# Seven block products for v of the second token group, computed ahead of the attention

## The chip, the cores and the metric

One Trainium2 (trn2) chip, one core. The metric is the device time of one launch in microseconds; the kernel before takes 2644.64 us (median of 3 runs, 2640.68 to 2646.3).

## The reference

One layer of a bidirectional encoder over 1024 prompt tokens and 256 sample tokens (1280 rows of `D_MODEL` = 2048), all in fp32:

```python
hn = rmsnorm(x, norm_w)
proj = hn @ w_in                    # 9232 columns
# na_q, na_k, na_v, na_g: 1024 each; ml_qk: 2048; ml_v, ml_o, ml_z: 1024 each; 16 gate columns
att = neighbourhood_attention(na_q, na_k, na_v, na_rpb)      # 8 heads x 128, grid 64 wide, window 8 x 16
att = att * silu(na_g)
...
ml = bidirectional_mlstm(q, k, ml_v, gates)                  # 4 heads x 256, chunks of 64
...
y = x + concat(att, ml) @ w_out
out = rmsnorm(y, final_w)
```

What matters here are the 2048 columns of v (`na_v` and `ml_v`) and the 16 gate columns, for the second part of the tokens.

## The kernel before, in words

**Precision.** Every large product is made of three matmuls on a split operand: `hi` is a cast (ScalarE, L153), `lo` the rest (VectorE, L154), and hi.hi, hi.lo and lo.hi are summed in PSUM. So each tile of weights costs one ScalarE and one VectorE instruction before TensorE can use it.

**Tokens.** The 1280 tokens form two groups: group 0 with 768 (`GA`), group 1 with 512 (`GB`).

**Stages.** The *first stage* projects group 0: `pair_a` (L328) makes two blocks of 128 output columns by seven block products (a Strassen scheme) with 384 token columns, and GpSimd makes the four weight sums that the scheme needs (products 6, 3, 7 and 5; function `summed` in `pair_a`; tile names like `A60t`, four buffers). Eight of the pairs are v. Free time of GpSimd goes to the sums of `w_out` (`wsum`, stored to `sD`). The *second stage* projects group 1 by ordinary products: `proj_pair` (L503; 96 matmuls of 512 token columns to a pair, PSUM tiles `pc`, weight pieces `wr`, split tiles `ws`) for q, k, gates and the mLSTM columns, and `proj_v` (L565; 192 matmuls of 256 v columns to a unit, PSUM tiles `pv`, outputs `vo`) for the eight units of v. Unit 4 carries the 16 gate columns besides, in matmuls of 272 columns. The *output stage* multiplies with `w_out`, again by seven products (groups S, G00, G01, G10, G11 in the profile), and normalizes.

**Order of the second stage.** The loop at L1170 takes one head group `i` of four after the other: `proj_v(4 + i)`, two mLSTM pairs, `proj_v(i)`, the q and k pairs, and then, by `run`, the mLSTM and attention units of that group (names `mlp3...` for the prompt's mLSTM head 3, `nap7...` for the prompt's attention head 7, `nas...` and `mls...` for the sample). `run` gives its instructions a high priority; a scheduler fixes the order of each engine when the kernel is built, and puts the low-priority projections of later groups into the attention's gaps. Behind the loop come the late gates: for `ch` in 0, 2, 4, 6 `late_gate(OT0 + ch, 8 + ch)` (pairs 40 and 48, 42 and 50, 44 and 52, 46 and 54) followed by `build` of the output stage's operands (`bd0...`, split into `cm0...`), and then `late_gate(GT0 + h, h)` (pairs 16, 18, 20, 22). A late gate multiplies its columns into `mixT` (`mx...`), where the attention and the mLSTM have stored their outputs.

**Queues.** SyncE (SP) issues nearly all loads and stores in program order, one behind the other; a store that waits for its data holds all loads behind it.

```python
for i in range(ML_H):
    proj_v(4 + i, X)
    if i == 0:
        x_stats(1, lambda c: mid(f"xdg1_{c}", 256))
    for n in (QK0 + 8 + 2 * i, QK0 + 2 * i):
        proj_pair(n, X)
    ...
    proj_v(i, X)
    for n in (QT0 + 2 * i, KT0 + 2 * i):
        proj_pair(n, X)
    run(...)
```

Of the kernel before, what the change touches and what calls it, by code (L numbers as in the profile page):

```python
# [11 lines left out]
ALU = mybir.AluOpType  # L12
# [20 lines left out]
BIAS_S = 6 * NAK  # L33
XFIRST = (0, 1, 8, 9, 2, 3, 10, 11, 4, 5)
QT0, KT0, GT0, QK0, OT0, ZT0 = 0, 8, 16, 24, 40, 48
# [3 lines left out]
def kernel(  # L39
# [6 lines left out]
    w_o: bass.AP,  # L46
    w_os: bass.AP,
    lnw: bass.AP,
    rpb_tab: bass.AP,
# [20 lines left out]
    pT = [dram.tile([P, TT], F32, tag=f"pT{n}", name=f"pT{n}") for n in range(NCH)]  # L70
    vD = [dram.tile([TT, 256], F32, tag=f"vD{u}", name=f"vD{u}") for u in range(NU)]
    mixT = [dram.tile([P, TT], F32, tag=f"mx{k}", name=f"mx{k}") for k in range(KT)]
# [106 lines left out]
    rbs = [xa.tile([P, GA], F32, tag="rstdb0", name="rstdb0"), None]  # L179
    XSLOT = {2: (0, 0), 3: (0, 1), 6: (1, 0), 5: (1, 1), 4: (2, 0), 7: (2, 1)}  # L180

# [13 lines left out]
    def wsa(name):  # L195
        return wa.tile([P, 2, 256], F32R, tag="wsa", name=name, bufs=NWS)
# [131 lines left out]
    def pair_a(n1, bg=iter(()), hook=None, units={}):  # L328
# [32 lines left out]
        for r in range(4):  # L361
# [8 lines left out]
            def summed(i, x, y_, op):  # L370
                t = wa.tile([P, 256], F32, tag="wt", name=f"{nm}t{r}{i}", bufs=NWT)
                G.tensor_tensor(t, x, y_, op=op)
# [110 lines left out]
    def po(name):  # L483
        return wb.tile([P, 520], F32, tag="po", name=name, bufs=NPO)
# [79 lines left out]

    def proj_v(u, X):  # L565
        gates = u == NA_H // 2
        w = 272 if gates else 256
        nt = GB // P
        if gates:
            outs = [bank("a", f"pv{u}_{i}")[:, :w] for i in range(nt)]  # L570
        else:
            pb = [bank("pr", f"pv{u}_{i}") for i in range(nt // 2)]
            outs = [pb[t // 2][:, (t % 2) * 256 : (t % 2) * 256 + 256] for t in range(nt)]
        for r in range(4):
            raw = w_piece(w_in[NCH // 2 + u, r], f"v{u}_{r}")
            rawv = raw.rearrange("p (j f q c) -> p f q j c", j=2, f=2, q=2)
            if gates:
                graw = wb.tile([P, 2, 2, 16], F32, tag="wgr", name=f"wg{r}", bufs=2)
                DM.dma_start(
                    graw, w_g.rearrange("p (f r q c) -> p f r q c", f=2, r=4, q=2)[:, :, r]  # L580
                )
            for f_ in range(2):
                t = wb.tile([P, 2, 544], F32R, tag="wsp", name=f"wsv_{u}_{r}_{f_}", bufs=4)
                t4 = t[:, :, : 2 * w].rearrange("p h (k c) -> p h k c", k=2)
                h2, l2 = (
                    t4[:, z, :, 0:256].rearrange("p q (j c) -> p q j c", j=2) for z in range(2)
                )
                split(h2, l2, rawv[:, f_])
                if gates:
                    split(t4[:, 0, :, 256:272], t4[:, 1, :, 256:272], graw[:, f_])  # L590
                for tt in range(nt):
                    for q in range(2):
                        first, last = r + f_ + q == 0, r == 3 and f_ == 1 and q == 1
                        xh, xl = X.get(8 * f_ + 2 * r + q)
                        for m, (xs, wi) in enumerate(((xh, 0), (xh, 1), (xl, 0))):
                            PE.matmul(  # L596
                                outs[tt],
                                xs[:, tt * P : (tt + 1) * P],
                                t[:, wi, q * w : (q + 1) * w],
                                start=first and m == 0 and (gates or tt % 2 == 0),  # L600
                                stop=last and m == 2 and (gates or tt % 2 == 1),
                            )
        rc = rcs[1]
        for tt in range(nt):
            o = po(f"vo{u}_{tt}")[:, :256]
            S.mul(o, outs[tt][:, :256], rc[:, tt : tt + 1])
            r0 = GA + tt * P
            DM.dma_start(vD[u][r0 : r0 + P, :], o)
            if gates:
                V.scalar_tensor_tensor(  # L610
                    gt[:, GA // P + tt, :], outs[tt][:, 256:272], rc[:, tt : tt + 1], gb_sb,
                    op0=ALU.mult, op1=ALU.add,
                )

# [531 lines left out]

    class LazyX:
        def __init__(self):
            self.t = {}

        def get(self, k):
            if k not in self.t:
                self.t[k] = x_split(x_raw(wb, 520, "po", NPO, 1, k), k, 1)
            return self.t[k]

    def run(*streams):
# [10 lines left out]

    X = LazyX()
    rbs[1] = late.tile([P, GB], F32, tag="rstdb1", name="rstdb1")
    for i in range(ML_H):  # L1170
        proj_v(4 + i, X)
        if i == 0:
# [18 lines left out]
    WBLK = {1: (0, 0), 4: (1, 1), 2: (0, 1)}  # L1191
    WSUM = {6: 0, 3: 1, 7: 2, 5: 3}

# [135 lines left out]

    def add(o, a_, b_):  # L1330
        V.tensor_tensor(o, a_, b_, op=ALU.add)

    PARTS = {
# [83 lines left out]
def _layout(inputs):  # L1417
# [8 lines left out]
    for name, n in (("q", 1024), ("k", 1024), ("v", 1024), ("g", 1024), ("qk", 2048),  # L1426
# [6 lines left out]
        ch.reshape(2, 4, 2, P, nb // 2, 2, P).transpose(4, 1, 3, 5, 0, 2, 6).reshape(nb // 2, 4, P, 1024)  # L1433
    )
    gorder = [d * 8 + w_ * 4 + h for w_ in range(2) for d in range(2) for h in range(4)]
    w_g = np.ascontiguousarray(
# [13 lines left out]
    def table(qr, qc, kr, kc, rows):  # L1450
# [22 lines left out]
        "w_o": w_o,  # L1473
        "w_os": w_os,
        "lnw": np.ascontiguousarray(g["ln_w"][0].reshape(KT, P).T),
        "rpb_tab": tab,
# [30 lines left out]
```

## Time and profile before

| what | us |
|---|---|
| median of 3 runs | 2644.64 |
| the profiled execution | 2650.84 |
| its span in the trace | 2649.1 |
| TensorE busy | 2592.8 |
| VectorE busy | 1989.0 |
| ScalarE busy | 1386.2 |
| GpSimd busy | 819.0 |
| first stage | 0 to 1122 |
| second stage | 1122 to 2224 |
| output stage | 2224 to 2649 |

The granted TensorE clock of the profiled execution is 0.996. The stage borders are the starts of the first matmul on `pv` and of the first on `G00p`. A busy time counts matmuls to their modelled ends, so that TensorE can be shown busy while it waits a little between two matmuls; its pace is better read from the chain, which gives the number of matmuls in each uninterrupted piece.

### The profile page before, as it was taken

How to read it: one execution, taken by the hardware profiler on the slowest of the kernel's cores; microseconds unless marked ns; L12 is line 12 of the kernel's file. 1: busy time of each engine (PE TensorE's matmuls, PEld its weight loads, DVE VectorE, ACT ScalarE, POOL GpSimd, SP SyncE). 2: the span in 40 equal slices, each digit the busy share in tenths (PEclk: the TensorE clock that was granted, in tenths of full speed). 3: DMA queues.
4: the chain of work that ended last, by engine and by line, in shares of the span. 5: the costliest groups of instructions: out<-in, count | busy, mean ns of one | idle time of the engine just before them, and what ended most of it. 6: DMA issues, size and time to landing. Idle time of an engine off the chain costs nothing.

```text
span 2649.1 us, 43618 instructions
## 1 busy us (share of the span) xinstructions
PE 2592.8 (98%) x14518; PEld 2372.1 (90%) x14518; DVE 1989.0 (75%) x3962; ACT 1386.2 (52%) x3140; POOL 819.0 (31%) x1021
## 2 busy tenths in 40 slices
PE   8999999999999999999999999999999999999997
PEld 8899999999999999988999998989888878877786
DVE  7868878897879798874587587587567675787775
ACT  7534434444444444443566566576566443565654
POOL 0546565756566565410011011011011000124312
PEclk9999999999999999999999999999999999999999
DMA  6524344434343343544555656656555456778875
GB/s 209 180 92 147 124 156 134 158 97 171 106 148 123 126 148 117 184 133 143 189 163 184 197 162 191 188 161 186 170 172 168 157 171 227 227 252 307 288 221 179
DMA packets 245753, 454.20 MB, mean 171 GB/s; under 512 B 30320, under 2 KB 121624, under 8 KB 245528
## 3 DMA queue, kind: packets, MB, share of 16 engines
q1 hardware_dynamic: 232856, 407.38, 48.0%
q0 software_dynamic: 9216, 33.56, 3.6%
q10 hardware_dynamic: 3456, 10.49, 1.0%
q8 instruction: 114, 1.87, 0.3%
q14 instruction: 111, 0.91, 0.1%
HBM read 368.41 MB, written 82.91 MB: 170 GB/s over the span
## 4 chain that ended last, share of the span: by engine, by line
PE 47%; DMA 5%; DVE 3%; ACT 2%; issue 1%; POOL 1%; SPq 0%; ACTq 0%; POOLq 0%; DVEq 0%
PE pc L514 20%; PE pv L596 4%; PE G00p L1286 3%; PE G11p L1286 3%; PE S L1286 2%; PE G10p L1286 2%; PE G01p L1286 1%; PE A54b L190 1%; PE A52b L190 1%; DMA wr<-in_w_in_dram 1%; PE nap_1s L638 1%; PE nap_0s L638 1%; DMA nap_0vr<-vD 1%; DMA wrG10w<-sD 0%; PE mlp_2in L942 0%
## 5 line engine op out<-in xcount | busy, mean ns | idle before, releaser
L154 DVE TENSOR_TENSOR ws<-wr,ws 128x512 fp32r<-128x512 f32 x224 | 155.2, 697 | 115.0 <-ACT ws L153 114.2
L153 ACT CAST ws<-wr 128x512 fp32r<-128x512 f32 x224 | 137.5, 619 | 158.2 <-PE pc L514 118.3
L1309 POOL TENSOR_TENSOR y<-y,fn 128x512 f32<-128x512 f32 x40 | 62.5, 1577 | 413.5 <-ACT jk L1308 216.9
L104 POOL TENSOR_SCALAR mls_0r<-mls_0r 128x2 f32<-128x2 f32 x4 | 1.1, 277 | 255.7 <-ACT mls_0jk L1110 255.7
L154 DVE TENSOR_TENSOR ws_S<-wrS,ws_S 128x512 fp32r<-128x512 f32 x64 | 54.8, 884 | 15.6 <-ACT ws_S L153 15.4
L154 DVE TENSOR_TENSOR wsv<-wr_v,wsv 128x512 fp32r<-128x512 f32 x64 | 44.5, 698 | 21.4 <-ACT wsv L153 20.9
L153 ACT CAST wsv<-wr_v 128x512 fp32r<-128x512 f32 x64 | 39.3, 617 | 36.1 <-PE pc L514 21.9
L154 DVE TENSOR_TENSOR ws_G10w<-wrG10w,ws_G10w 128x512 fp32r<-128x512 f32 x56 | 45.2, 830 | 13.5 <-ACT ws_G10w L153 13.2
L1286 PE MATMUL S<-ws_S,xsb 128*128 128x512 f32 x192 | 48.3, 406 | 5.0 <-DVE ws_S L154 3.9
L153 ACT CAST ws_G11w<-wrG11w 128x512 fp32r<-128x512 f32 x56 | 34.6, 620 | 33.2 <-PE G11p L1286 16.4
L154 DVE TENSOR_TENSOR ws_G11w<-wrG11w,ws_G11w 128x512 fp32r<-128x512 f32 x56 | 43.0, 793 | 11.2 <-ACT ws_G11w L153 11.2
L154 DVE TENSOR_TENSOR ws_G01w<-wrG01w,ws_G01w 128x512 fp32r<-128x512 f32 x56 | 45.1, 828 | 7.9 <-ACT ws_G01w L153 6.7
L1286 PEld LDWEIGHTS S<-ws_S,xsb 128*128 128x128 f32 x192 | 36.8, 194 | 15.7 <-DVE ws_S L154 6.0
L167 DVE TENSOR_TENSOR pco<-pc,rstdb 128x512 f32<-128x512 f32 x48 | 32.9, 687 | 23.5 <-PE pc L514 23.4
L153 ACT CAST ws_S<-wrS 128x512 fp32r<-128x512 f32 x64 | 37.9, 617 | 20.6 <-PE S L1286 11.5
L276 DVE SCALAR_TENSOR_TENSOR pcv<-pco,cw_sb,pcv 128x516 f32<-128x516 f32 x64 | 47.7, 754 | 0.9 <-ACT pcv L270 0.8
L319 POOL DMA_DIRECT2D wsum<-in_w_os_dram x32 | 18.5, 577 | 96.4 <-DVE xg L161 77.5
L514 PE MATMUL pc<-x_2h,ws 128*128 128x512 f32 x112 | 44.8, 400 | 2.2 <-ACT ws L153 1.1
L153 ACT CAST ws_G10w<-wrG10w 128x512 fp32r<-128x512 f32 x56 | 33.9, 619 | 24.7 <-PE G10p L1286 11.0
L153 ACT CAST ws_G01w<-wrG01w 128x512 fp32r<-128x512 f32 x56 | 34.2, 618 | 22.7 <-PE G01p L1286 12.4
L153 ACT CAST ws_G00w<-wrG00w 128x512 fp32r<-128x512 f32 x48 | 29.4, 620 | 31.0 <-PE G00p L1286 17.3
L154 DVE TENSOR_TENSOR ws_G00w<-wrG00w,ws_G00w 128x512 fp32r<-128x512 f32 x48 | 36.3, 775 | 12.4 <-ACT ws_G00w L153 11.7
(1824 smaller groups left out, 9342.7 us busy)
## 6 DMA issues: line engine op xcount, KB each, us to landing
wr<-in_w_in_dram SPq DMA_DIRECT2D x112, 512.0 KB
wsum<-in_w_os_dram POOLq DMA_DIRECT2D x32, 512.0 KB, 4.4
sD<-wsum POOLq DMA_DIRECT2D x32, 512.0 KB, 3.3
wr_v<-in_w_in_dram SPq DMA_DIRECT2D x32, 512.0 KB
wrS<-in_w_o_dram SPq DMA_DIRECT2D x64, 256.0 KB
xq<-in_xtok_dram SPq DMA_DIRECT2D x20, 512.0 KB
xr<-in_xtok_dram SPq DMA_DIRECT2D x40, 256.0 KB
wrG00w<-sD SPq DMA_DIRECT2D x32, 256.0 KB
```

The costliest lines, as they stand in the source:

```text
L104: E.tensor_scalar(out, ssum, 1.0 / count, EPS, op0=ALU.mult, op1=ALU.add)
L153: S.copy(hi, src)
L154: V.tensor_tensor(lo, src, f(hi), op=ALU.subtract)
L167: V.tensor_tensor(o, src, rb, op=ALU.mult)
L190: PE.matmul(o, w(a_), x(b_), start=first and m == 0, stop=last and m == 2)
L276: V.scalar_tensor_tensor(dst[:, a:n], src[:, a + j - pad : n + j - pad], cw_sb[:, ct, j : j + 1], dst[:, a:n], op0=ALU.mult, op1=ALU.add,)
L319: G.dma_start(raw, w_os[u])
L514: PE.matmul(pb[j], t[:, wi, c : c + P], xs, start=r == 0 and f_ == 0 and q == 0 and wi == 0 and xs is xh, stop=r == 3 and f_ == 1 and q == ...
L596: PE.matmul(outs[tt], xs[:, tt * P : (tt + 1) * P], t[:, wi, q * w : (q + 1) * w], start=first and m == 0 and (gates or tt % 2 == 0), stop ...
L638: PE.matmul(b[:, :nkeys], qs(a_), ks(b_), start=i == 0, stop=i == 2)
L1286: PE.matmul(bk[s_], x_[:, xi, s_ * P : (s_ + 1) * P], t[:, wi, :512], start=first and m == 0, stop=last and m == 2,)
L1309: G.tensor_tensor(yc, yc, fn[nb], op=ALU.mult)
```

## The change: what it does

`proj_v` is gone. Its work is done in a new stage between the first stage and the loop, by seven block products over two column groups `cp` of 1024 columns:

- The first stage's v pairs store the four weight sums that GpSimd makes anyway to `sV` (128 stores of 128 KB through SP's queue).
- `v_build`, eight times, loads two tiles of x again, scales them (ScalarE), makes the token sums of the scheme with four instructions on GpSimd, and splits them.
- `v_product`, 7 x 2 times, runs 48 matmuls of 512 columns (tiles named `V` with group and product). Products 1, 4 and 2 read plain weights from a new input `w_vb`, which holds the same weights in this order; 6, 3, 7 and 5 read `sV`.
- `v_fold` adds the products, `v_out` scales by the row statistics and stores to `vG`; `vD[u]` is now a slice of it.
- `v_gates` makes the 16 gate columns: 32 matmuls of 512 token columns (only 32 rows of the result are used) and four small ones that bring them into token order.
- The x tiles of group 1 that are loaded early (`XFIRST`) are 0 to 9 instead of 0, 1, 8, 9, 2, 3, 10, 11, 4, 5.

The core of the diff:

```diff
+                if n1 >= NCH and i in WSUM:
+                    u = (n1 - NCH) // 2
+                    DM.dma_start(
+                        sV[u // 4][:, WSUM[i], 2 * r : 2 * r + 2, u % 4],
+                        src[i].rearrange("p (q c) -> p q c", q=2),
+                    )
...
+    def v_build(kk):
+        nm = f"vb{kk}"
+        s0, s1 = (po(f"{nm}{z}")[:, :GB] for z in range(2))
+        for z, s_ in enumerate((s0, s1)):
+            k = kk + 8 * z
+            DM.dma_start(s_, xT[:, k, GA : GA + GB])
+            S.mul(s_, s_, lnw_sb[:, k : k + 1])
+        b11, b12, d1, t3 = s0[:, :QB], s0[:, QB:], s1[:, :QB], s1[:, QB:]
+        G.tensor_tensor(s1, s1, s0, op=ALU.subtract)
+        G.tensor_tensor(b12, b12, b11, op=ALU.subtract)
+        G.tensor_tensor(b11, t3, b11, op=ALU.add)
+        G.tensor_tensor(d1, d1, t3, op=ALU.subtract)
+        for kind, src in (("v", s0), ("w", s1)):
+            t = vp.tile([P, 2, GB], F32R, tag=f"{kind}{kk}", name=f"{nm}{kind}")
+            split(t[:, 0], t[:, 1], src)
+            vx[kind, kk] = t
...
+    def v_product(cp, i):
+        tag = "pr" if count["bank"] % 3 == 0 else "a"
+        count["bank"] += 1
+        bk = [bank(tag, f"V{cp}{i}_{s_}") for s_ in range(2)]
+        for kk, t in v_tiles(cp, i):
+            for s_ in range(2):
+                for m, (xi, wi) in enumerate(((0, 0), (0, 1), (1, 0))):
+                    PE.matmul(
+                        bk[s_], v_op(i, kk, xi, s_), t[:, wi, :512],
+                        start=kk == 0 and m == 0, stop=kk == 7 and m == 2,
+                    )
+        return bk
...
+    todo = list(range(8))
+    for i in (1, 2, 3):
+        for cp in range(2):
+            v_fold(cp, i, v_product(cp, i))
+            if (cp, i) == (0, 1):
+                for k in range(8, KT):
+                    X.get(k)
+            for kk in todo[: 2 if (cp, i) != (0, 1) else 0]:
+                v_build(kk)
+            del todo[: 2 if (cp, i) != (0, 1) else 0]
+    v_gates()
+    for cp in range(2):
+        for i in (6, 5, 7, 4):
+            v_fold(cp, i, v_product(cp, i))
+    v_ctx.close()
...
     for i in range(ML_H):
-        proj_v(4 + i, X)
         if i == 0:
             x_stats(1, lambda c: mid(f"xdg1_{c}", 256))
...
-        proj_v(i, X)
         for n in (QT0 + 2 * i, KT0 + 2 * i):
             proj_pair(n, X)
```

In the loop the scheduler has fewer low-priority instructions to place between the attention's. Three places show it; line numbers of the changed kernel are higher (its L524 is L514 of before, L157 is L154, L892 and L900 are L764 and L772, L501 is L491, L905 is L777, L1324 is L1210).

TensorE at the end of the attention. In before, the last attention product (`nap7_3o`: prompt, head 7, fourth row block) stands amid matmuls of pair 46:

```order
L514 MATMUL pc46_1_24699<-x1_9h_12633,ws_46_01_24717 128x512
L514 MATMUL pc46_0_24698<-x1_2h_12669,ws_46_10_24734 128x512
L764 MATMUL nap7_3o_23712<-nap7_3pt_23684,nap7_3v_23648 128x256 x5
L764 MATMUL nap7_3o_23712<-nap7_3pt_23684,nap7_3v_23648 128x128 x6
L514 MATMUL pc46_0_24698<-x1_2l_12670,ws_46_10_24734 128x512
L514 MATMUL pc46_0_24698<-x1_2h_12669,ws_46_10_24734 128x512
```

Behind it in before still come the rest of pair 46 and the pairs 54, 16, 18, 20 and 22. In the changed kernel, pair 54 ends within head 6:

```order
L524 MATMUL pc54_1_24544<-x1_15h_12860,ws_54_31_24658 128x512
L783 MATMUL nap6_2_1t_22412<-ident_175,nap6_2_1st_22277 128x128 x3
L892 MATMUL nap6_1o_22418<-nap6_1pt_22291,nap6_1v_22167 128x256 x6
...
L892 MATMUL nap7_2o_23406<-nap7_2pt_23365,nap7_2v_23284 128x128 x6
L892 MATMUL nap7_3o_23421<-nap7_3pt_23393,nap7_3v_23357 128x256 x6
L892 MATMUL nap7_3o_23421<-nap7_3pt_23393,nap7_3v_23357 128x128 x6
L524 MATMUL pc16_0_24729<-x1_0h_12691,ws_16_00_24733 128x512
```

From the last matmul of pair 54 to the first of pair 16 there are 365 matmuls, all of the attention and the mLSTM.

VectorE at the same place of the changed kernel: `ws_54_31` is the last split of pair 54's weights, `nap7o` the output of head 7, `cm0...` and `bd0...` the operands of the output stage, `ws_16_00` the first weight tile of pair 16:

```order
L157 TENSOR_TENSOR ws_54_31_24658<-wr_54_3_24641,ws_54_31_24658 128x512
L771 ISA nap6_2_0st_22265,nap6_2_0sm_22266<-nap6_2_0s_22259,nap6_2_0bt_22263 128x384
...
L786 TENSOR_TENSOR nap7_3pt_23393<-nap7_3_1t_23400,nap7_3pt_23393 128x3x128
L900 SCALAR_TENSOR_TENSOR nap7o_22690<-nap7_3o_23421,nap7o_22690 128x12x16
L157 TENSOR_TENSOR cm0u7_24714<-bd0b7_24710,cm0u7_24714 128x512
L157 TENSOR_TENSOR cm0b0_23728<-bd0b0w6_23725,cm0b0_23728 128x256
...
L1345 TENSOR_TENSOR bd0b0w6_23725<-bd0b0w6_23725 128x256
L157 TENSOR_TENSOR ws_16_00_24733<-wr_16_0_24731,ws_16_00_24733 128x512
```

Between the two `ws` rows stand 249 instructions, 235 up to the last `nap7o` and 14 on the operands. In before the splits of pair 46's last tiles, of pair 54 and of pair 16 follow `nap7o`, mixed with the operands'.

SP's queue around the store of head 7's output (`mx7` is written from `nap7o`), in the changed kernel:

```order
L573 DMA mx15_138<-pco54_1_24675 128x512
L905 DMA mx7_130<-nap7o_22690 128x1024
L1324 DMA bd0b0w6_23725<-mx0_123 128x512
L1324 DMA bd0b0w6_23725<-mx8_131 128x512
L1324 DMA bd0b1w7_23744<-mx1_124 128x512
L1324 DMA bd0b1w7_23744<-mx9_132 128x512
L1324 DMA bd0b7_24710<-mx7_130 128x512
L501 DMA wr_16_0_24731<-in_w_in_dram 128x1024
```

In before the store stands behind the loads of pair 46 and of the first piece of pair 54 (`wr_54_0`), and the pieces of pair 54 and of pair 16 follow it; in the changed kernel the first piece behind the store is pair 16's.

More of the change, by code (lines that the diff above doesn't have):

```diff
@@ L47 @@
     w_os: bass.AP,
+    w_vb: bass.AP,
     lnw: bass.AP,
@@ L563, in late_gate @@
             DM.dma_start(mixT[k][:, GA:], z_)
[L565 to L580, printed above, removed]
-                )
[L582 to L613, printed above, removed]
@@ new lines, with __init__, get @@
+    class LazyX:
+        def __init__(self):
+            self.t = {}
+        def get(self, k):
+            if k not in self.t:
+                self.t[k] = x_split(x_raw(wb, 520, "po", NPO, 1, k), k, 1)
+            return self.t[k]
+    X = LazyX()
+    rbs[1] = late.tile([P, GB], F32, tag="rstdb1", name="rstdb1")
+    v_ctx = ExitStack()
+    vp = v_ctx.enter_context(tc.tile_pool(name="vp", bufs=1))
+    QB = GB // 2
+    vx = {}
+    def v_build(kk):
[14 more added lines that the diff above has]
+            vx[kind, kk] = t
@@ new lines, in vt, with v_out, add @@
+    def vt(tag, name, bufs):
+        return vp.tile([P, 512], F32, tag=tag, name=name, bufs=bufs)
+    def v_out(cp, s_, c_, t_, o):
+        t = 2 * t_ + s_
+        S.mul(o, o, rcs[1][:, t : t + 1])
+        r0 = GA + t * P
+        DM.dma_start(
+            vG[cp][r0 : r0 + P, :].rearrange("p (u j c) -> p j u c", j=2, c=P)[:, c_],
+            o.rearrange("p (u c) -> p u c", c=P),
+        )
+    def add(o, a_, b_):
+        V.tensor_tensor(o, a_, b_, op=ALU.add)
+    vU, vA, vU5 = {}, {}, {}
@@ new lines, in v_gates @@
+    def v_gates():
+        raw = vt("vo", "vgw", 4)
+        DM.dma_start(raw[:, :256], w_g)
+        st = vp.tile([P, 16 * 32 + 96], F32R, tag="vgs", name="vgs")
+        G.memset(f(st[:, 512:]), 0.0)
+        tv = st[:, :512].rearrange("p (k h c) -> p k h c", h=2, c=16)
+        split(tv[:, :, 0, :], tv[:, :, 1, :], raw[:, :256].rearrange("p (k c) -> p k c", c=16))
+        sel = raw[0:32, 256:272]
+        V.tensor_tensor(sel, ident[0:32, 0:16], ident[0:32, 16:32], op=ALU.add)
+        b = bank("a", "vgb")
+        for k in range(KT):
+            for hl_ in range(2):
+                PE.matmul(
+                    b, st[:, k * 32 : k * 32 + P], X.get(k)[hl_],
+                    start=k + hl_ == 0, stop=k == KT - 1 and hl_ == 1,
+                )
+        gs = vt("vo", "vgg", 4)
+        V.tensor_copy(gs[0:32], b[0:32])
+        b = bank("a", "vgt")
+        for tt in range(GB // P):
+            PE.matmul(
+                b[:, tt * 16 : tt * 16 + 16], gs[0:32, tt * P : (tt + 1) * P], sel,
+                start=True, stop=True,
+            )
+            V.scalar_tensor_tensor(
+                gt[:, GA // P + tt, :], b[:, tt * 16 : tt * 16 + 16], rcs[1][:, tt : tt + 1], gb_sb,
+                op0=ALU.mult, op1=ALU.add,
+            )
@@ L1144, in ml_units @@
             yield out_unit(J)
[L1147 to L1154, printed above, removed]
     def run(*streams):
```

72 lines of the change are left out of this document (65 added, 7 removed).

## Prediction, made before the changed kernel ran

> **What bounds the kernel now.** I read the page's busy shares first, then the chain of work that ended last, then the sums of busy time over stretches of the span, then single tiles and the timeline around the end of the attention.
>
> ```profile
> PE 2592.8 (98%) x14518; PEld 2372.1 (90%) x14518; DVE 1989.0 (75%) x3962; ACT 1386.2 (52%) x3140; POOL 819.0 (31%) x1021
> ...
> 1093.26 29.13 PE A54b L190 x168
> 1122.39 9.01 PE pv L596 x72
> ...
> 1138.63 8.76 PE pv L596 x68
> ...
> 1201.49 16.89 PE pv L596 x143
> ...
> 1224.68 41.73 PE pc L514 x180
> ...
> 2162.60 61.54 PE pc L514 x264
> 2224.14 77.49 PE G00p L1286 x336
> ...
> 2413.38 58.20 PE S L1286 x244
> ```
>
> The first line says that TensorE (PE) is the bound on the average. The chain gives its pace, stage by stage: start, duration, group, number of matmuls. A matmul of 384 columns in the first stage takes 29.13/168 = 0.173 us. In the second stage the v units' matmuls take 16.89/143 = 0.118 us (256 columns) and 9.01/72 = 0.125 us (272, the unit with the gate columns), the pairs' 41.73/180 = 0.232 us (512 columns). In the output stage 512 columns take 77.49/336 = 0.2306 us where the weights keep up, and 58.20/244 = 0.2385 us in product S. The price goes by columns, so the change must be counted in columns, not in instructions.
>
> **The products themselves.** Removed are seven v units of 192 matmuls of 256 columns and one of 192 of 272 columns: 1344 x 0.118 + 192 x 0.125 = 158.7 + 24.0 = 182.8 us. Added are seven products in two column groups, 8 x 2 x 3 = 48 matmuls of 512 columns each, 672 in all; they have the form of the output products, so 672 x 0.2306 = 155.0 us. The gates add 32 matmuls of 512 columns (7.4 us, although only 16 columns are wanted) and four small ones (4 x 0.12 = 0.5). PE's work changes by 155.0 + 7.4 + 0.5 - 182.8 = **-19.9 us**.
>
> One rule speaks against counting so. The Trainium skill (TensorE: Matmul & The Clock Gate, Back-to-back issue gap) gives a sustained spacing of about 81 ns at 128 columns and 131 ns at 512, so that width would cost little and the wide form would win some 60 us (an estimate from that page's figures); the rows above, 0.118 against 0.232, show the price nearly doubling with the width.
>
> **The rest of the v stage.** It must be fed: two megabytes of weights per product and column group, 14 times, the x tiles twice and the stores, 29 + 8 + 4 = some 42 MB in 163 us, 256 GB/s. VectorE (DVE) splits 112 weight tiles, 16 x tiles and 16 sums, and folds 28 banks: 172 x 0.69 = 119 us, 73% of the stage.
>
> ```profile
> L154 DVE TENSOR_TENSOR ws<-wr,ws 128x512 fp32r<-128x512 f32 x224 | 155.2, 697 | 115.0 <-ACT ws L153 114.2
> ...
> L154 DVE TENSOR_TENSOR ws_S<-wrS,ws_S 128x512 fp32r<-128x512 f32 x64 | 54.8, 884 | 15.6 <-ACT ws_S L153 15.4
> ```
> ```profile
> 2224.00:2340.00 116.00, 116.00 (x505) 94.54 (x504) 85.45 (x126) 60.76 (x112) 13.16 (x8) 1.00 0.79 257
> 2350.00:2500.00 150.00, 143.57 (x601) 112.66 (x600) 120.14 (x158) 94.58 (x174) 72.00 (x65) 0.99 0.82 275
> ```
>
> The columns of the last two rows are the stretch, its length, then busy time of PE, PEld, DVE, ACT and POOL, the granted clock, the DMA share and GB/s. The first of them is the nearest row: 257 GB/s, DVE 74% busy, and PE still at 0.2306 us with no idle time. So I take the stage at its matmuls alone. The start costs a stall in both kernels: in the chain the first unit ends at 1131.4 and the next piece of it starts at 1138.63, 7 us in which PE mostly waits for x tiles and pieces. Afterwards the second half of x and the first pieces stand in SP's queue as they do now. I take 0 for the difference, bounds -5 (the gap goes) and +10 (it more than doubles, since the sums' x loads and the last stores of the first stage share the queue).
>
> **The first stage's stores.** GpSimd's (POOL) sums for the eight v pairs are stored, 128 stores of 128 KB on SP's queue, and each of the four sum buffers comes free only when its store has been read out.
>
> ```profile
> L372 POOL TENSOR_TENSOR A60t<-A60r 128x256 f32<-128x256 f32 x8 | 8.5, 1066 | 6.8 <-DVE A60s L161 6.0 <-DVE A28s L161 0.7
> ```
> ```profile
> sD<-wsum POOLq DMA_DIRECT2D x32, 512.0 KB, 3.3
> ```
>
> A quarter of a pair lasts 29.13/4 = 7.3 us and makes one sum per buffer; POOL waits for buffers already (6.8 us before 8 sums), ahead of its readers. A store of 512 KB lands in 3.3 us, inside 7.3. Behind a store in SP's queue stands the next weight piece, loaded three deep. I take 0; bounds 0 and 32 us (1 us for each of 32 pieces).
>
> **What the moved work uncovers.** This is the term that decides. The v units were also filler: 182.8 us of matmuls without dependence on the attention, which PE ran while DVE and ScalarE (ACT) worked on it. The order shows that the remaining pairs are then used up too early: after pair 54 stand 365 matmuls of the attention and nothing else, and then pair 16. Pair 16 can't move up: its pieces stand in SP's queue behind the store of the last head's output, its tiles behind the late gates before it.
>
> ```profile
> 1980.00:2094.00 114.00, 114.00 (x640) 99.35 (x639) 83.75 (x229) 67.96 (x167) 8.94 (x16) 1.00 0.49 153
> 2020.00:2050.00 30.00, 30.00 (x179) 26.71 (x178) 24.19 (x81) 20.12 (x53) 1.78 (x4) 1.00 0.46 139
> ```
> ```profile
> 1980.00:2094.00 114.00, 82.28 (x332) 60.30 (x331) 18.84 (x27) 16.61 (x27) 1.00 0.49 153
> ```
> ```profile
> 1980.00:2094.00 114.00, 13.03 (x19) 4.29 (x7) 0.00 (x0) 1.00 0.49 153
> ```
>
> These are the last head pair of before: all work; the same for a crowded part of it; then the weight tiles alone (PE, PEld, DVE, ACT); then the pairs' outputs alone (DVE, ACT, POOL). PE's 332 wide matmuls take 332 x 0.232 = 77 us of the 114, so 308 matmuls of the attention take 37, 0.120 each. DVE's own work for the attention is 83.75 - 18.84 - 13.03 = 51.9 us in 229 - 27 - 19 = 183 instructions, 0.283 each: 1.4 times PE's. Nothing waits today because half of PE's time is filler.
>
> Of the changed kernel, the 365 matmuls are 365 x 0.120 = 43.9 us. On DVE stand 235 instructions between the split of pair 54's last weight tile and the last piece of the attention's output: 235 x 0.283 = 66.6 us. From that split PE has the 43.9 and between one and four weight tiles of 12 matmuls (2.8 to 11.1 us), about 51 in the middle. If DVE never idles it ends 66.6 - 51 = 16 us behind; if it is as busy as in the crowded stretch, 24.19/30 = 81%, it needs 82 and ends 31 behind. I take **22**. Bounds: 0 (DVE ran ahead during pair 54), and 91, by the attention's present pace (114 x 365/308 = 135 us, less 43.9).
>
> Then comes the handover.
>
> ```profile
> 2093.10 0.35 DVE L772 SCALAR_TENSOR_TENSOR nap7o<-nap_3o,nap7o 128x192 f32<-128x192 f32 x1
> ...
> 2093.72 0.32 SPq L777 DMA_DIRECT2D mx<-nap7o  x1
> ...
> 2099.06 0.80 SPq L1210 DMA_DIRECT2D bd0b0w<-mx  x2
> 2099.91 0.90 SPq L1210 DMA_DIRECT2D bd0b1w<-mx  x2
> ```
> ```profile
> 2093.72 5.26 DMA mx<-nap7o
> ...
> 2122.77 4.06 DMA bd0b4w<-mx
> ...
> 2157.43 4.42 DMA wr<-in_w_in_dram
> ```
>
> In before PE works on pairs 46 and 54 through all of this. Afterwards it waits: 0.6 us to the store, 5.3 until the store has landed and SP goes on (2093.72 to 2099.06), 1.7 for the loads of the output stage's operands, 0.4 for one more of them (first half of the last head's output), then pair 16's first piece, 8.0 us after DVE's last output; it lands 4.4 later, at 12.4. Ahead of its split DVE has 14 instructions on those operands, which themselves land at 7.6 + 4.1 = 12 or so: 14 x 0.6 = 8.4, so the first weight tile of pair 16 is ready near **21 us**. Bounds 12 (only the loads count) and 30 (the two transfers as slow as the store, and the wait from PE to DVE before the first).
>
> **The sum.** -19.9 + 0 + 0 + 22 + 21 = +23 us on the profiled execution's 2650.84, so 2674; the median shown is 2644.64, 6.2 us below, so **2668 us**. The output stage is unchanged; it starts later by as much. On DVE and ACT the stages where the v units stood get looser, which nothing waits for.
>
> **The rivals.** In terms of the uncovered time X, the median becomes 2624.7 + X.
> First, *faster*: the cover holds. DVE can take the attention's scores early, while pair 54 still runs, and if it is some 16 us ahead when PE leaves pair 54, only the loads' 12 us remain: X = 12, 2637 us. For it speaks that the order puts attention matmuls among pair 54's too; against it, that DVE's 66.6 us stand behind the split which those matmuls need. It decides at X = 20: a lead of DVE of 23 us.
> Second, *about no change*: a lead of half that, X = 15 to 25, 2640 to 2650 us.
> Third, the v stage runs like product S instead of the row with 257 GB/s, with POOL's sums beside it (ws_S 884 ns against 697): 672 x (0.2385 - 0.2306) = 5.3 us, and idle time at the rate of 2350 to 2500, 6.43/150 x 163 = 7.0, together +12: 2680 us.
> Fourth, the first stage's stores hold its pieces: +32, 2700 us.
> Fifth, the attention without filler goes at its present pace because each of its steps waits for the one before: X = 91 + 21, 2737 us. Against it: in 2020 to 2050 two heads already overlap and DVE is 81% busy.
> Sixth, a matmul costs the same at either width: 704 x 0.118 = 83 us against 182.8, 80 us less than in my sum, 2588 us; the rows of 256 and 512 columns speak against it. The Trainium skill's two figures (TensorE: Matmul & The Clock Gate, Back-to-back issue gap) lie between that and the rows.
>
> **How the numbers follow.** My forecast has 0.51 (with X 27 to 65, 2652 to 2690), the third rival 0.13, the fourth 0.07, the fifth 0.05: slower 0.76. The second has 0.11. The first has 0.12, the sixth 0.01: faster 0.13. A measurement of this kernel can tell about 0.2%, 5.3 us, from no change; the bounds are 2639.4 and 2649.9. The range runs from 2636, just below the first rival, to 2702, just above the fourth; what is left out is the sixth, the fifth and the outer parts of first and fourth, less than 0.2.
>
> **What would show it.** Right: the v products' 672 matmuls at 0.231 each in about 163 us; the first stage's end within a few us of 1122; PE idle or thin for some 20 us in the attention after pair 54's last matmul while DVE is nearly full; then a gap of about 20 us without matmuls ahead of pair 16, in the chain as the last head's store, operand loads and DVE splits. Wrong: a first stage that ends 10 or more us late (fourth rival), v products at 0.238 or with gaps for weights (third), PE busy through the end of the attention (first), or DVE idle there while PE waits as well (fifth).

## The result, and the profile after

The changed kernel takes 2719.84 us (median of 4 runs, 2716.9 to 2731.55), beside 2645.47 us for the kernel before in the runs taken with it: 1.0291 times as long, interval 1.0257 to 1.0325, or 74 us more. I had forecast 2668 us and a range up to 2702. The direction was right, the size too small by a factor of three.

The lines of the page and of the chain of waits that answer to those of before:

```profile
PE 2597.5 (96%) x13694; PEld 2332.9 (86%) x13694; DVE 2060.2 (76%) x4049; ACT 1436.5 (53%) x3205; POOL 853.8 (31%) x1054
```
```profile
1090.93 14.57 PE A54b L194 x84
...
1236.24 70.75 PE V L646 x306
1306.99 11.11 PE pc L524 x48
...
2182.11 2.60 DMA mx<-nap7o
2186.15 4.16 DMA bd0b1w<-mx
...
2243.84 50.35 PE pc L524 x216
2294.19 77.49 PE G00p L1400 x336
...
2483.27 56.62 PE S L1400 x244
```

The chain gives the pace and the borders. The new products run at 70.75/306 = 0.231 us where nothing holds them, as forecast. The first product of the output stage starts at 2294.19 instead of 2224.14, 70.0 us later, and from there to the end the two kernels are alike (2717.7 - 2294.2 = 423.5 against 2649.1 - 2224.1 = 425.0). So everything happened in the second stage. The new stage ends at 1307.0, 184.6 us after the start of the second stage before (1122.4); I had 162.9. From there to the output stage are 987.2 us; the same part of before, without its units, is 1101.8 - 182.8 = 919.0, so the uncovered time is 68.2 us; I had 43. With -19.9 of work, the parts are 21.7 beyond the v stage's matmuls and 68.2 uncovered, together 70.0. They add up by definition, so the sum alone proves nothing about the causes.

The busy times in some stretches (start:end, length, then PE, PEld, DVE, ACT, POOL, clock, DMA share, GB/s) show where the time went:

```profile
1120.00:1180.00 60.00, 43.13 (x167) 30.72 (x166) 53.26 (x59) 42.82 (x74) 38.38 (x35) 0.91 0.75 246
1180.00:1307.00 127.00, 126.80 (x549) 102.02 (x548) 77.66 (x123) 62.87 (x104) 1.00 (x1) 1.00 0.64 191
```
```profile
2081.60:2181.40 99.80, 66.42 (x395) 60.03 (x393) 66.78 (x216) 58.41 (x160) 8.94 (x16) 0.81 0.37 114
2086.52:2181.50 94.98, 61.54 (x365) 55.59 (x363) 64.00 (x209) 55.35 (x152) 8.94 (x16) 0.80 0.39 117
```
```profile
2180.00:2196.00 16.00, 3.38 (x13) 2.78 (x12) 8.12 (x17) 5.46 (x11) 0.00 (x0) 0.50 0.46 164
```

First: the v stage loses its time in its first 60 us, where VectorE is 89% busy and GpSimd works: 16.9 us in which TensorE has nothing, and matmuls at a lower clock (0.91 in the mean); after 1180 nothing is lost. In the same stretch of before TensorE is never without work for long:

```profile
1120.00:1180.00 60.00, 59.67 (x385) 53.35 (x384) 44.70 (x107) 28.40 (x49) 6.64 (x23) 1.00 0.45 149
```

What TensorE waited for there in the changed kernel (us, times, the longest), and VectorE's weight splits while GpSimd makes the sums (1140 to 1180) and after them (1185 to 1307):

```profile
PE V L646 <- ACT ws_V L156: 9.1, 1, 9.1
PE V L646 <- DVE ws_V L157: 7.8, 8, 2.2
```
```profile
L157 DVE TENSOR_TENSOR ws_V<-vrV,ws_V 128x512 fp32r<-128x512 f32 x21 | 26.3, 1294 | 6.5 <-ACT ws_V L156 6.4
L157 DVE TENSOR_TENSOR ws_V<-vrV,ws_V 128x512 fp32r<-128x512 f32 x80 | 54.7, 690 | 42.8 <-ACT ws_V L156 41.5 <-DMA vrV<-sV 0.7
```

The same split takes 1.29 us beside GpSimd's sums and 0.69 without them, so the 21 splits alone cost VectorE 12.7 us more. The single wait of 9.1 us is of another kind: VectorE itself stands still in it for 6.0 us. The weights with which it ends are loaded from 1136.16 on, after SP has waited for the first stage's last output to be stored (`pT<-A54c`, until 1136.08), and cast at 1139.6.

Second: the end of the attention. Pair 54's last matmul ends at 2086.5, the last attention product at 2181.4. Between them stand the 365 matmuls, 43.8 us at the 0.120 of before, in 95 us (the second of the two rows), so 51 are lost. TensorE is empty for 33.4 of them; in the rest it runs the matmuls more slowly, at a mean clock of 0.80. VectorE's work is what I had counted, from the last split of pair 54 on (66.8 us in the first row, against 66.6), but it is only 67% busy, and no other engine is full. Third: the handover, in which PE has next to nothing.

What PE waited for in the second and third part, in us, times, and the longest (the first five):

```profile
PE pc L524 <- ACT ws L156: 12.6, 1, 12.6
PE mlp_1in L1070 <- ACT mlp_1Cf L156: 11.8, 1, 11.8
PE mlp_2in L1070 <- DVE mlp_0zr L1259: 4.4, 1, 4.4
PE mlp_3tp L1245 <- DVE mlp_3hs L1243: 4.2, 1, 4.2
PE mlp_0in L1070 <- ACT mlp_0Cb L156: 2.4, 1, 2.4
```

The first row is the handover to pair 16: 12.6 us, where I had 21. The others belong to the attention's end, and but for the 11.8 none is large: the mLSTM's steps wait for states that are cast, for loads, and for each other. The chain of waits from the end of pair 54 to the last product runs 27 us through transfers, 25 through VectorE, 21 through TensorE (95 matmuls) and 14 through ScalarE. Four of its pieces (start, duration):

```profile
2110.80 4.23 DMA mlp_3vr<-vG
2116.94 3.48 DMA mlp_3qcv<-cD
...
2174.60 2.62 PE nap_2o L892 x11
2178.84 2.62 PE nap_3o L892 x11
```

The first two lie in the wait of 11.8 us. In before TensorE is busy through the whole of its last head pair (114.00 of 114.00 us in the row ahead of the result).

### The profile page after: what moved, and what is told of

Same layout as the page of the kernel before. It is cut to its first block, busy times and chain, and to the rows that moved or that the text cites. A ratio compares the mean times of both kernels' runs of the same rounds, so it can differ in the third digit from the quotient of the medians.

```text
span 2717.7 us, 42750 instructions
## 1 busy us (share of the span) xinstructions
PE 2597.5 (96%) x13694; PEld 2332.9 (86%) x13694; DVE 2060.2 (76%) x4049; ACT 1436.5 (53%) x3205; POOL 853.8 (31%) x1054
## 4 chain that ended last, share of the span: by engine, by line
PE 41%; DMA 8%; DVE 6%; ACT 3%; issue 2%; SPq 1%; POOL 0%; ACTq 0%; POOLq 0%; DVEq 0%
PE pc L524 17%; PE V L646 4%; PE G00p L1400 3%; PE G11p L1400 3%; PE S L1400 2%; PE G10p L1400 2%; DMA wr<-in_w_in_dram 1%; PE G01p L1400 1%; DMA nap_0vr<-vG 1%; PE A52b L194 1%; DMA xr<-in_xtok_dram 1%; PE A54b L194 1%; PE nap_0s L766 1%; PE nap_2o L892 0%; PE nap_1s L766 0%
## 5 line engine op out<-in xcount | busy, mean ns | idle before, releaser
L157 DVE TENSOR_TENSOR ws<-wr,ws 128x512 fp32r<-128x512 f32 x224 | 155.4, 698 | 77.6 <-ACT ws L156 76.1
L157 DVE TENSOR_TENSOR ws_V<-vrV,ws_V 128x512 fp32r<-128x512 f32 x104 | 83.0, 812 | 49.3 <-ACT ws_V L156 47.9
L156 ACT CAST ws_V<-vrV 128x512 fp32r<-128x512 f32 x104 | 64.1, 618 | 59.8 <-PE V L646 52.0
L157 DVE TENSOR_TENSOR ws_S<-wrS,ws_S 128x512 fp32r<-128x512 f32 x64 | 54.9, 891 | 13.4 <-ACT ws_S L156 13.4
L524 PE MATMUL pc<-x_0h,ws 128*128 128x512 f32 x112 | 45.5, 407 | 13.2 <-ACT ws L156 12.6
L157 DVE TENSOR_TENSOR ws_G10w<-wrG10w,ws_G10w 128x512 fp32r<-128x512 f32 x56 | 45.3, 832 | 13.2 <-ACT ws_G10w L156 13.0
L157 DVE TENSOR_TENSOR ws_G11w<-wrG11w,ws_G11w 128x512 fp32r<-128x512 f32 x56 | 43.0, 792 | 11.2 <-ACT ws_G11w L156 11.2
L157 DVE TENSOR_TENSOR ws_G01w<-wrG01w,ws_G01w 128x512 fp32r<-128x512 f32 x56 | 45.0, 826 | 8.3 <-ACT ws_G01w L156 6.5
L524 PE MATMUL pc<-x_4h,ws 128*128 128x512 f32 x112 | 46.0, 410 | 3.1 <-ACT ws L156 2.9
L1400 PEld LDWEIGHTS S<-ws_S,xsb 128*128 128x128 f32 x192 | 35.6, 188 | 15.3 <-DVE ws_S L157 6.0
L524 PE MATMUL pc<-x_6h,ws 128*128 128x512 f32 x112 | 45.0, 402 | 1.2 <-ACT ws L156 1.2
```

Source lines behind the costliest of these rows:

```text
L156: S.copy(hi, src)
L157: V.tensor_tensor(lo, src, f(hi), op=ALU.subtract)
L524: PE.matmul(pb[j], t[:, wi, c : c + P], xs, start=r == 0 and f_ == 0 and q == 0 and wi == 0 and xs is xh, stop=r == 3 and f_ == 1 and q == ...
L1400: PE.matmul(bk[s_], x_[:, xi, s_ * P : (s_ + 1) * P], t[:, wi, :512], start=first and m == 0, stop=last and m == 2,)
```

## The experiments

Two theories stood against each other: A, that the filler taken away (the v units) is what the attention's end misses, and B, that the new stage or its stores cost the time. Times are medians; the changed kernel is 2720, the kernel before 2646.0 to 2648.5 in the four sets of runs. The changed kernel was not run again in these sets, and its own four runs lie between 2716.9 and 2731.6, so a difference of some 6 us from it says little.

**The late gates earlier.**

```diff
     for ch in range(0, 8, 2):
+        if ch == 6:
+            for h in range(0, 6, 2):
+                late_gate(GT0 + h, h, X)
         late_gate(OT0 + ch, 8 + ch, X)
...
-    for h in range(0, NA_H, 2):
-        late_gate(GT0 + h, h, X)
+    late_gate(GT0 + 6, 6, X)
```

> The changed kernel with the same work, but the late gates of pairs 16, 18 and 20 (attention heads 0 to 5) written ahead of pairs 46 and 54, so that the order has no longer any stretch of attention without a projection pair beside it (before this edit: 365 matmuls). Theory A (the missing filler at the attention's end costs about 73 of the 74 us, the rest of the change nets to zero): 60 to 70 us faster than the changed kernel, 2650 to 2660 us. Rival B (the v stage or the first stage's stores cost it, the end of the attention is slow for another reason such as the new layout of v): about as slow as the changed kernel, 2710 to 2720 us.

Measured: 2687.5 us, 1.0151 of before (1.0136 to 1.0167): 32 us back, half of what A said, so A's number failed, and B is out. The busy times in the last two stretches before its output stage (same columns) show where the other half is:

```profile
2207.00:2220.00 13.00, 0.89 (x2) 0.80 (x3) 6.08 (x13) 4.84 (x10) 0.00 (x0) 0.50 0.65 222
2220.00:2260.00 40.00, 33.57 (x119) 23.84 (x118) 33.44 (x65) 19.21 (x35) 0.00 (x0) 0.86 0.79 260
```

The attention is now covered, but only pair 22 is left behind it, so the handover (13 us empty) and the operands of the output stage stand open instead. The reordering moved the hole as well as shrinking it.

**Useless work as filler.**

```diff
+    for n in (QT0, KT0, QT0 + 2):
+        proj_pair(n, X, True)
     for ch in range(0, 8, 2):
```

> The changed kernel with three projection pairs more (3 x 96 matmuls of 512 columns, 67 us of matmuls), whose results nobody reads, ahead of the late gates. Theory A: TensorE runs them in time in which it waits now, so at most 15 us more than the changed kernel, 2720 to 2735 us. Rival B: 67 us more, 2787 us.

Measured: 2746.4 us, 26.6 us more than the changed kernel for 66.7 us of added matmuls, with their loads and splits. So 40 us of useless work went in for nothing, and 27 did not, more than A allowed: the attention itself ends later with a pair beside it (its last output is stored at 2211 us instead of 2182).

**The stage priced by itself, and its stores.** The old units put back beside the new stage (the removed lines of the diff, restored), and in the kernel before only the `sV` stores added.

> The changed kernel with the eight v units of before put back at their places too, so that v of group 1 is computed twice, by the new stage and by the old units; output the same. It prices the new stage, stores included, with the old filler in place. Theory A: 163 us by my sum, or 183 to 190 by the lengths in the trace of the changed kernel, on top of 2645: 2810 to 2835 us. Rival B: 183 + 74 = 257 us on top: 2900 us.

> The kernel before with only the 128 stores of weight sums in the first stage added; nothing reads them. Theory A and my prediction: within 3 us of 2645. Rival B in the form of my fourth rival: 2677 us.

Measured: 2835.1 us with both, 187.6 above before, at the upper end of A's range: the new stage costs what its length in the changed kernel's trace says (from its first matmul at 1119.89 to 1306.99, 187.1 us), 25 us more than its matmuls. Its attention reads v from the new layout too, so with the old filler in place the layout costs nothing that shows. The reverse reading is as useful: from this kernel to the changed one 182.8 us of units are taken out, and 115.3 come back. The stores alone: 2645.1 us, ratio 0.9993 (0.9983 to 1.0002), nothing.

**Half of the change.** Column group 1 by seven products, the attention's half by four units as before; the eight builds stand behind products 2 and 3 in the program.

```diff
-        for cp in range(2):
+        for cp in (1,):
             v_fold(cp, i, v_product(cp, i))
...
+        proj_v(i, X)
         for n in (QT0 + 2 * i, KT0 + 2 * i):
             proj_pair(n, X)
```

> Half of the change: only the mLSTM's half of v (column group 1) is made by seven products in the new stage, 336 matmuls of 512 columns; the attention's half stays with four of the old v units (768 matmuls of 256 columns, 91 us) at their old places in the loop. The first stage still stores all sums, of which half are read. Theory A (filler is missed only once it is used up before the attention ends): the four removed units save nearly their whole 91 us, the half stage costs 77 + 8 of matmuls and some 20 of losses at its start: 2647 - 91 + 105 = 2660, between 2652 and 2668 us. Rival C (every removed unit gives back only the share that all eight gave back, 115 of 183 us): 2647 - 57 + 105 = 2695, between 2687 and 2702 us.

Measured: 2665.8 us, 1.0066 (1.0049 to 1.0084), as A said and 21 us below C's range. In its chain the stage ends, and the pairs begin, at 1227.23, 104.8 us after 1122.4, so 2648.5 - 91 + 105 = 2662 if the four units had given back all of their 91 us: nearly all of it. Four units could go at nearly no loss of cover; all eight could not. The chain's row, and the busy times at the attention's end, which is nearly closed:

```profile
1227.23 11.13 PE pc L524 x48
```

```profile
2100.00:2180.00 80.00, 73.64 (x340) 58.26 (x339) 57.21 (x117) 37.39 (x78) 0.85 (x2) 0.98 0.47 148
```

**The start of the v stage.** Once the second product's weights through the other buffers (`if i == 1:` for `if (cp, i) == (0, 1):`), once without the token sums:

```diff
-            for kk in todo[: 2 if (cp, i) != (0, 1) else 0]:
-                v_build(kk)
...
-        return vx[kind, kk][:, hl_, c * QB + s_ * P :][:, :P]
+        return X.get(kk)[hl_][:, QB + s_ * P :][:, :P]
```

> The changed kernel, but the second product of the new stage takes its weights through the buffers that the first one uses (they lie outside the first stage's memory, and their loads stand ahead of the last stores of the first stage and of the x loads for the sums). Theory D (the 9 us wait at that product is for its weights, whose buffers lie in memory that the first stage still reads): 7 to 10 us faster than the changed kernel, 2710 to 2713 us. Rival E (VectorE is full there anyway, so the wait only moves): 2716 to 2721 us.

> The changed kernel without the token sums: the eight builds (16 loads, 16 scalings on ScalarE, 32 instructions on GpSimd, 16 splits) are left out, and products 6, 5, 7 and 4 use a plain x tile in their place, so the computed v of group 1 is another. Theory E (the builds fill VectorE and GpSimd in the stage's first 60 us): 8 to 15 us faster than the changed kernel, 2705 to 2712 us. Theory D (the loads and the memory of the first stage set the start): within 4 us of it, 2716 to 2721 us.

Measured: 2719.3 us, no change, for the first (its v stage ends at 1304.00, only 3 us earlier); 2704.6 us, 15 us back, for the second. The first lies in E's range, the second 0.4 us below it, and both outside D's. The start of the stage without the sums, beside the row of 1120 to 1180 above:

```profile
1120.00:1180.00 60.00, 57.05 (x251) 46.26 (x250) 42.60 (x69) 36.24 (x60) 0.31 (x3) 1.00 0.84 271
```

251 matmuls instead of 167 in the same 60 us, at a higher transfer rate (271 against 246 GB/s), with weight splits of 0.690 us. So the builds cost the 15 us. Which part of them is shown only in part: the waits for splits are VectorE's, slowed beside GpSimd, but the edit takes away the builds' 16 loads as well, and what the 9.1 us wait owes to these loads and what to work stays open.

**The output stage's operands last.** `build` moved from the loop over `ch` into the loop over `h`, behind each `late_gate(GT0 + h, h, X)`; in the changed kernel, in the half change and in the kernel before.

> The changed kernel with the operands of the output stage built behind the late gates of pairs 16 to 22 in the program, two with each, instead of between the late gates of pairs 40 to 54; same work. In the order no stretch of the attention is left without a pair beside it, and only pair 22 comes behind it. Theory A (there is too little filler in all for the attention, its handover and the operands together): the hole moves to the start of the output stage, 2680 to 2695 us, as with the gates earlier. Rival F (only the place matters, there is filler enough): 2650 to 2665 us.

> The half change (four units kept) with the operands of the output stage built behind the late gates of pairs 16 to 22 as well. Theory A: around the attention's end the half change loses some 10 us more than the kernel before, and no more than that can come back: 2656 to 2666 us. Rival F (the place of the operands is worth by itself the 40 us that it gave in the changed kernel): 2625 to 2635 us.

> The kernel before with only that reordering of the operands. Theory A: nothing waits there, within 4 us of 2648. Rival F: 2608 to 2630 us.

Measured: 2678.4, 2653.2 and 2643.5 us; ratios to before 1.0116 (1.0100 to 1.0132), 1.0027 (1.0018 to 1.0037) and 0.9988 (0.9978 to 0.9998). The changed kernel gets 41 us back (1.6 below A's range), the half change 13 (3 more than A allowed; 10 by the two ratios to before, which leave out the difference between the sets), the kernel before 2.5 in its own set (half a us below A's range). F is out in all three: the edit is worth about what is open at that place. In the changed kernel part of the hole moved on, as A said: its first output product waits 8.6 us for ScalarE's casts of weights and 1.2 us for VectorE's splits. In the half change nothing is open any more around the attention's end (the last output is stored at 2129 us):

```profile
2050.00:2130.00 80.00, 79.89 (x456) 69.76 (x455) 53.67 (x153) 44.35 (x110) 4.39 (x10) 1.00 0.48 144
2130.00:2230.00 100.00, 100.00 (x434) 81.31 (x433) 71.23 (x128) 43.16 (x77) 0.00 (x0) 1.00 0.64 205
```

The kernel before with this edit has the lowest median of all, by 2.5 us, hardly more than a measurement tells from no change.

**The clock.** In the changed kernel the same twelve matmuls of an attention product take twice as long at the end as some 100 us earlier (start, duration, group); the granted clock is 1.00 around the first and 0.50 around the second:

```profile
2073.51 1.59 PE L892 MATMUL nap_0o<-nap_0pt,nap_0v 128*128 128x256 f32 x12
```
```profile
2178.16 3.28 PE L892 MATMUL nap_3o<-nap_3pt,nap_3v 128*128 128x256 f32 x12 [0.95 <-ACT nap_3pt L785]
```

So useless matmuls were put where PE waits, to hold the clock up (8 in one kernel, 20 in the other):

```diff
             b = bank("a", f"{n2}o")
+            if h >= 6:
+                for _ in range(8):
+                    PE.matmul(b, v[:, 0, 0:P], X.get(0)[0], start=True, stop=True)
```

> The changed kernel with 8 useless matmuls of 512 columns ahead of each attention product of heads 6 and 7 (8 row blocks; 64 in all, 14.8 us at the full clock, 56 of them in the stretch without a pair beside it); they need only that block's v, and their result is overwritten. They stand where TensorE waits for the softmax weights. Theory G (the clock that falls to 0.5 when TensorE idles lengthens the chain of the attention's end): the clock holds longer, and the kernel gets faster in spite of the work, 2705 to 2717 us. Rival H (the chain is set by VectorE, ScalarE and transfers; the clock costs nothing on it): the matmuls fit into the waits in part, 2720 to 2733 us.

> The same with 20 useless matmuls at each place, 160 in all, 37 us, 140 of them in the stretch without a pair. Theory G: no more than 5 us slower than the changed kernel. Rival H: 10 to 30 us slower, since 4.6 us at each place are longer than the waits of 1 to 3 us there.

Measured: 2725.7 and 2737.5 us, 6 us slower (hardly told from no change) and 18 us slower, for 14.8 and 37 us of work. Theory G falls as stated; both lie in H's ranges. The row over 2100 to 2180 of the changed kernel, then of the two:

```profile
2100.00:2180.00 80.00, 48.62 (x293) 43.95 (x294) 52.14 (x172) 46.36 (x126) 8.94 (x16) 0.81 0.40 122
```
```profile
2100.00:2180.00 80.00, 54.28 (x312) 49.32 (x312) 52.74 (x183) 46.98 (x128) 7.59 (x16) 0.81 0.40 124
```
```profile
2100.00:2180.00 80.00, 58.31 (x353) 52.41 (x352) 53.03 (x185) 48.03 (x134) 7.80 (x16) 0.87 0.39 117
```

With 20 the clock rises from 0.81 to 0.87 and VectorE does 53 us of work in the stretch instead of 52: the chain hardly got faster. With 8 the clock did not rise over this stretch. What the clock costs by itself is not separated by this, since the added matmuls stand in the way of the attention's. The chain gives an estimate: its 95 matmuls take 20.9 us, 0.220 each instead of 0.120, so some 9 of the 51 us (an estimate from these two paces). H's "costs nothing" is therefore not shown.

**SP's queue.** The loads of v by GpSimd instead of SyncE (`G.dma_start` for `DM.dma_start` in the attention's row block and in the mLSTM's load of v).

> The changed kernel with the attention's and the mLSTM's loads of v issued by GpSimd instead of SyncE, so that SP's queue holds about 5 issues less for each row block and the loads behind them no longer wait there. Theory J (the end of the attention waits for loads that stand behind others in SP's queue; the longest wait of TensorE there, 11.8 us, ends with a q load of the mLSTM that stands behind four v loads): 8 to 25 us faster than the changed kernel, 2695 to 2712 us. Rival K (latencies and VectorE's and ScalarE's work between the steps set it, the queue does not): within 5 us, 2715 to 2725 us.

Measured: 2914.9 us, 195 us slower. Both expectations failed, and the run does not answer its question: it replaced one queue by a worse one. The idle time of the engine that splits a row block's v, ahead of it, until the load was there (us, times), in this kernel and in the changed one:

```profile
  DMA nap_0vr<-vG: 78.6, 8
```
```profile
  DMA nap_0vr<-vG: 17.8, 8
```

These are the first row blocks of the eight heads: 10 us for each instead of 2. GpSimd issued a block's four loads one by one, with idle time before the second, third and fourth (us, times):

```profile
  issue: 79.7, 24
```

That is 3.3 us between two loads, where SyncE needs some 0.52 us for each issue; they landed 2.7 to 6.3 us after it. Whether the order of loads on SP sets the pace at the attention's end stays open; no run here takes another hardware queue.

**Both edits that helped.**

> Both edits that gave time back to the changed kernel in one: without the token sums (another v of group 1 is computed) and with the output stage's operands behind the late gates. Theory A (two separate losses, the sums at the start of the v stage, 15 us, and the missing filler at the attention's end, 41 us of it given back by the order): they add up, 2720 - 15 - 41 = 2664, between 2658 and 2670 us. Rival L (an earlier start of the attention only uses the filler up earlier, so that part of the 15 us is lost again): 2671 to 2679 us.

Measured: 2658.1 us, 62 us back; 15.3 and 41.4 had come back singly, 56.7. Against the kernel before of each set it is 64 beside 18 and 44. The two losses are separate and add up; L falls.

## Why the prediction was wrong, point by point

- **What bounds the kernel, and the price by columns**: right. 0.231 us for 512 columns was measured, so PE's work did fall by about 20 us, and the whole gain was spent elsewhere. The sixth rival is out, and so is, for this kernel, the Trainium skill's 131 ns (TensorE: Matmul & The Clock Gate, Back-to-back issue gap).
- **The first stage's stores at 0**: right; `stores_only` differs by less than 0.2%. The fourth rival is out.
- **"I take the stage at its matmuls alone", and 0 for its start, bounds -5 and +10**: wrong, 21.7 us. The step that failed is the use of VectorE's share over the whole stage (73%, "172 x 0.69 = 119 us"). The measured share is 89% in the first 60 us and 61% (77.66/127) in the rest: x splits, the sums' splits and the last outputs of the first stage all fall at the front, and there a weight split takes 1.29 us, not 0.69. Taking the sums away gave 15 us. A reading was wrong as well: the "7 us in which PE mostly waits" of before are a detour of the chain through other engines; TensorE is idle for 0.3 us between 1120 and 1180 there, so before had no stall to set against the new one. The third rival had the right price within 10 us, and the slow splits beside GpSimd, but the wrong place, since it spread the loss over the stage.
- **The handover at 21 us**: the mechanism is in the chain as forecast (store of head 7's output, operand loads, splits, first tile of pair 16), the wait measured 12.6, near the lower bound. The store landed in 2.60 us, not 5.3. And the 14 operand instructions did not stand behind the loads with 8.4 us of their own: VectorE did them as the loads landed, from 2185.74 to 2194.8, and TensorE began at 2194.06 on ScalarE's cast, before VectorE's first split.
- **The uncovered attention at 22 us**: the mechanism is right (`gates_earlier`, `useless_pairs`, `half_units`), the size wrong: 51 us in the stretch itself, and some 5 more around it (68.2 - 51 - 12.6). The step that failed reads "If DVE never idles it ends 66.6 - 51 = 16 us behind; if it is as busy as in the crowded stretch, 24.19/30 = 81%, it needs 82". VectorE's work was right to 0.2 us, but it was 67% busy, not 81 to 100%: without a pair beside it the attention is a chain of steps from engine to engine, with 27 us of transfers and 21 of matmuls at a lowered clock in it, and no engine is full. The clock's share, some 9 us by the estimate above, was a term that the sum did not have. The 81% came from a stretch with pairs beside it, which were just what would be missing. The fifth rival said so, for a price of 91, and its sign, VectorE idle while TensorE waits as well, is what the row shows; I gave it 0.05; the truth lies between, nearer to the middle than to my 22.
- **The range**: two terms were wrong in the same direction, by 25 and 22 us, and its upper end allowed for either alone.

Expectations behind the result were wrong as well. I thought that the order alone would bring back nearly all; it brought back 32 or 41 of 68, because the filler is short in sum: with the pairs used up inside the attention, the handover and the operands stand open. And I thought that filler costs nothing inside the attention; 66.7 us of it cost 26.6. Those for the clock's theory G and for the loads by GpSimd failed too.

## What to carry to other kernels

Work with no dependence beside a latency-bound stretch is worth less than its length: 182.8 us of such units came back as 115, and the stage that replaced them stood alone on the path with its full 188. Before such filler is made cheaper and moved ahead, count what is left of it at the end of the stretch it covers: half of it could go free here, the other half not. And a mean busy share says nothing of a stage whose side work falls into its first third; ask for it there, and price VectorE's instructions there beside what GpSimd does (1.29 us against 0.69 here).

## What the runs showed of the hardware

TensorE's granted clock drops to half within a few us of an empty PE and comes back as fast. In the changed kernel, around the wait of 11.8 us:

```profile
2108.00:2112.00 4.00, 1.91 (x16) 1.70 (x15) 3.03 (x13) 3.48 (x12) 0.00 (x0) 1.00 0.87 247
2112.00:2116.00 4.00, 0.00 (x0) 0.00 (x0) 3.21 (x9) 3.57 (x12) 0.98 (x2) 0.60 0.85 284
2116.00:2120.00 4.00, 0.00 (x0) 0.00 (x0) 1.36 (x4) 0.91 (x4) 0.00 (x0) 0.50 0.67 216
2120.00:2124.00 4.00, 2.30 (x10) 2.30 (x11) 2.56 (x4) 2.34 (x5) 2.61 (x4) 0.50 0.30 83
2124.00:2128.00 4.00, 3.29 (x17) 3.00 (x17) 2.26 (x7) 1.70 (x4) 0.61 (x1) 0.69 0.26 69
2128.00:2132.00 4.00, 3.73 (x29) 3.44 (x28) 2.89 (x11) 3.08 (x7) 0.00 (x0) 1.00 0.10 25
```

The clock column goes 1.00, 0.60, 0.50, 0.50, 0.69, 1.00. The Trainium skill (TensorE: Matmul & The Clock Gate, Part 1, What's actually happening) lists two states, full and half, set by windows of about 3.4 us; the rows agree, the values between being means over 4 us. I had not counted it at all. It makes the matmuls of a stretch in which PE often runs empty slower: 0.220 us each on the chain here, where the attention's matmuls of before took 0.120 in the mean.

A split of a 128x512 weight tile on VectorE takes 1.29 us while GpSimd makes the token sums and 0.69 us without them, in the same kernel; in the kernel without the sums all 34 of the same stretch take 0.690 us in the mean, at a higher transfer rate.

Loads issued by GpSimd stood 3.3 us apart within a row block, where SyncE takes some 0.52 us for an issue. The split of a head's first row block of v waited about 10 us where it had waited 2, and the kernel took 195 us more with the loads of 32 row blocks of the attention and of the mLSTM's v moved so.
